# Token chunks of 368, 368 and 352 columns instead of 364, 364 and 360 in a hybrid SSD and pooling decoder step

## The chip, the cores and the metric

The kernel runs on one core of one Trainium2 chip. The metric is device time in microseconds, from runs of the whole kernel; the profile is of one execution. Engines are TensorE (PE, with its weight loads as PEld), VectorE (DVE), ScalarE (ACT), GpSimd (POOL) and SyncE (SP), which issues most DMAs.

## The reference

One inference step of a two-layer decoder trunk, on a prompt of 1024 tokens and eight sampled sequences of 8 tokens each. All 1088 tokens go through the same weights, in float32.

```
for layer 0 (SSD) and layer 1 (pooling):
    shift, scale, gate = split(silu(c) @ ada_w + ada_b, 3)
    hn = rmsnorm(x) * (1 + scale) + shift
    layer 0: zxbcdt = hn @ w_in                    # 1024 -> 6176
             xbc = silu(causal_conv4(xbc))         # carries conv state
             y, state = ssd_scan(x, dt, A, B, C)   # 32 heads, state 128, chunks of 128
             out = (groupnorm(y * silu(z))) @ w_out        # 2048 -> 1024
    layer 1: u, z = split(hn @ w_in, 2)            # 1024 -> 2 x 2048
             pooled = window means of u (2, 4, 8, 16) - u
             mixed = (pooled @ w_group) * ch_scale * silu(z)   # 4 groups of 512 -> 512
             out = mixed @ w_out                   # 2048 -> 1024
    x = x + (1 + gate) * out
y = rmsnorm(x)
```

It returns y for prompt and samples and the new SSM, convolution and pooling states.

## The kernel before, in words

Everything is held transposed: channels on the 128 partitions, the 1088 tokens along the free dimension, first the 1024 of the prompt, then the 64 of the samples. Every float32 operand of the large products is split into a high part `hi` in the reduced format fp32r and a rest `lo` in the same format, and a product of 128 input by 128 output channels is three matmuls, issued by the helper `mm1` (L182 to L184), the weights standing and the tokens streaming:

```
nc.tensor.matmul(ps[:, :n], hi[:, k, :], ah[:, a:a + n], start=first, stop=False)
nc.tensor.matmul(ps[:, :n], hi[:, k, :], al[:, a:a + n], start=False, stop=False)
nc.tensor.matmul(ps[:, :n], lo[:, k, :], ah[:, a:a + n], start=False, stop=last)
```

A PSUM tile holds at most 512 columns, so the tokens are cut into the three chunks of the constant `CH` (L20); `mm3` runs `mm1` over all input tiles k (8 or 4) of one chunk, and the chunk is then evicted. Chunk 2 ends in the 64 sample columns, which are evicted separately.

Large products come in two kinds. The *plain* ones use `CH`. The *fast* ones (`product`, L980 to L982, in `fast_pair`; and `op_half`, L1196 to L1198, in `out_product`) are a seven-product scheme on half blocks, whose streams are always a quarter of the tokens, 272 columns; they do not use `CH`. What uses `CH`:

- `front`: the first four gate tiles of the SSD input projection (8 steps of k each), the squares and the modulation of its first input tile.
- `proj_group`: 20 tiles of the SSD input projection for the groups in `BESIDE` (8 steps each). They are generators that `ssd_layer` steps between pieces of the scan (`scan_group`), by the hand-written counts in `FILL`; `proj_evict` (L419) copies a chunk out with ScalarE.
- `op_units` and `last_part`: the first output projection in four parts of four input tiles, 8 output tiles each (4 steps each); parts 0 to 2 also fill the scan's gaps. `op_unit` (L764) adds each chunk to the residual with VectorE.
- `ssd_out`: by chunk, the norm and the modulation for the second layer (`modulate`).
- `plain_pairs`: four tiles of the pooling layer's input projection (8 steps each).
- `pool_mix`: the 16 tiles of the mixer (4 steps each); L1096 multiplies a chunk into the gate.

The plain products' PSUM tiles are of the tag `mm` with three buffers (in `plain_pairs` also `y`). In the scan, `states` (L588) and `rows` (L609, L613) are TensorE's other work, and L663 runs the samples' state products, 512 columns wide in the same reduced format. The order of the engines' queues follows the order of these generators, with `issue_after` edges where the code gives one.

Of the kernel before, what the change touches and what calls it, by code (L numbers as in the profile page):

```python
# [16 lines left out]
NS = 64  # L17
TOK = NP + NS
HALF, QUART = TOK // 2, TOK // 4
CH = ((0, 364), (364, 364), (728, 360))  # L20
KD = 8
EPS = 1e-6
GROUPS = (1, 2, 3, 0)
# [74 lines left out]
class Build:  # L98
# [288 lines left out]
    def proj_group(self, G):  # L387

        for ii in range(4):
            w = self.stream_next()  # L390
            raw = self.proj_begin(G, ii)
            if (G["g"], ii) == (BESIDE[-1], 3):

                ps = [self.mm_tile() for _ in CH]
                for k in range(8):
                    for c in range(3):
                        self.mm1(ps[c], w, k, self.hn[k], CH[c], k == 0, k == 7)
                    self.slots.free(*self.hn[k])
# [9 lines left out]
            for c in range(3):  # L408
                ps = self.mm_tile()
                self.mm3(ps, w, self.hn, CH[c])  # L410
                self.proj_evict(G, ii, raw, ps, c)
# [4 lines left out]
    def proj_evict(self, G, ii, raw, ps, c):  # L416
        nc, (a, n) = self.nc, CH[c]
        pn = min(a + n, NP) - a
        nc.scalar.activation(raw[:, 3 + a:3 + a + pn], ps[:, :pn], AF.Identity)  # L419
        if pn < n:  # L420
            nc.scalar.activation(raw[:, 1027:1115].rearrange("p (b w) -> p b w", w=11)[:, :, 3:11],
                                 ps[:, pn:n].rearrange("p (b i) -> p b i", i=8), AF.Identity)
            self.proj_end(G, ii, raw, True)

    def gate_chunk(self, dst, c, ps):

        return self.z_chunk(dst, ps[:, :CH[c][1]], *CH[c])

# [343 lines left out]
    def sq_add(self, ss, x, d, first, a=0, n=TOK, eng=None):  # L772
        nc = self.nc
        eng = eng or nc.gpsimd
        if first:
            nc.scalar.activation(ss[:, a:a + n], x[:, a:a + n], AF.Square)
            return
        for b, m in CH if n == TOK else ((a, n),):
            t = self.gp2.tile([P, HALF], F32, tag="mt2", bufs=self.nmt2, name=self.name("sq"))
# [1027 lines left out]
```

## Time and profile before

| | us |
|---|---|
| runs before, median of 3 (lowest, highest) | 1631.87 (1627.06, 1631.94) |
| profiled execution, span from first to last instruction | 1632.2 |
| PE busy in it | 1601.1 (98%) |
| PEld busy | 1524.7 (93%) |
| DVE busy | 1290.3 (79%) |
| ACT busy | 816.7 (50%) |
| POOL busy | 495.2 (30%) |

For the profiled execution there is no other time than its span. Busy time counts an instruction from its start to a modelled end, and matmuls overlap in it; what a matmul takes of TensorE is read from the distance between starts. A row of the timeline has the start in us, the length in us, the engine, the line, the operation, the tile written and those read, and the shapes.

### The profile page before, as it was taken

How to read it: one execution, taken by the hardware profiler on the slowest of the kernel's cores; microseconds unless marked ns; L12 is line 12 of the kernel's file. 1: busy time of each engine (PE TensorE's matmuls, PEld its weight loads, DVE VectorE, ACT ScalarE, POOL GpSimd, SP SyncE). 2: the span in 40 equal slices, each digit the busy share in tenths (PEclk: the TensorE clock that was granted, in tenths of full speed). 3: DMA queues.
4: the chain of work that ended last, by engine and by line, in shares of the span. 5: the costliest groups of instructions: out<-in, count | busy, mean ns of one | idle time of the engine just before them, and what ended most of it. 6: DMA issues, size and time to landing. Idle time of an engine off the chain costs nothing.

```text
span 1632.2 us, 30956 instructions
## 1 busy us (share of the span) xinstructions
PE 1601.1 (98%) x12061; PEld 1524.7 (93%) x12061; DVE 1290.3 (79%) x2140; ACT 816.7 (50%) x1565; POOL 495.2 (30%) x527
## 2 busy tenths in 40 slices
PE   8999999999999999999999999999999999999997
PEld 6899999998899888988998899999999999999997
DVE  6875779777788888789887867988889867577876
ACT  6653334456776767575645536632322333333364
POOL 0233556511221202121212222366667640000241
PEclk9999999999999999999999999999999999999999
DMA  9422232264555554668898533043333369565783
GB/s 346 163 98 84 93 109 71 105 203 133 183 162 167 165 186 135 217 232 299 276 332 284 201 137 111 29 142 112 102 112 99 129 213 367 166 170 173 167 164 119
DMA packets 122306, 275.60 MB, mean 169 GB/s; under 512 B 18192, under 2 KB 59312, under 8 KB 122160
## 3 DMA queue, kind: packets, MB, share of 16 engines
q1 hardware_dynamic: 118128, 260.91, 46.8%
q0 software_dynamic: 4032, 12.72, 4.5%
q8 instruction: 95, 1.56, 0.4%
q14 instruction: 51, 0.42, 0.1%
HBM read 201.12 MB, written 70.23 MB: 166 GB/s over the span
## 4 chain that ended last, share of the span: by engine, by line
PE 82%; DVE 7%; DMA 5%; issue 3%; ACT 2%; POOL 1%; SPq 0%; DVEq 0%; ACTq 0%; POOLq 0%
PE st L982 11%; PE st L980 11%; PE st L981 11%; PE mm L182 10%; PE mm L184 10%; PE mm L183 10%; DMA acb<-acd 2%; PE op L1197 2%; PE op L1198 2%; PE op L1196 2%; PE y L609 2%; PE S L588 2%; PE y L613 2%; PE am L253 1%; PE tr L549 1%
## 5 line engine op out<-in xcount | busy, mean ns | idle before, releaser
L982 PE MATMUL st<-hh,w 128*128 128x272 f32 x832 | 240.8, 289 | 2.3 <-DVE w L176 2.3
L980 PE MATMUL st<-hh,w 128*128 128x272 f32 x832 | 240.2, 289 | 0.0
L981 PE MATMUL st<-hl,w 128*128 128x272 f32 x832 | 239.7, 288 | 0.0
L982 PE MATMUL st<-t,w 128*128 128x272 f32 x624 | 179.6, 288 | 0.0
L980 PE MATMUL st<-t,w 128*128 128x272 f32 x624 | 179.6, 288 | 0.0
L981 PE MATMUL st<-t,w 128*128 128x272 f32 x624 | 179.2, 287 | 0.0
L182 PE MATMUL mm<-hh,wh 128*128 128x364 f32 (+1 forms) x528 | 178.4, 338 | 0.1
L184 PE MATMUL mm<-hh,wl 128*128 128x364 f32 (+1 forms) x528 | 174.6, 331 | 0.0
L183 PE MATMUL mm<-hl,wh 128*128 128x364 f32 (+1 forms) x528 | 173.7, 329 | 0.0
L174 ACT ACTIVATE w<-wr 128x512 fp32r<-128x512 f32 x104 | 65.6, 631 | 190.4 <-PE st L982 156.8
L982 PEld LDWEIGHTS st<-hh,w 128*128 128x128 f32 x832 | 156.4, 188 | 3.4 <-DVE w L176 3.4
L980 PEld LDWEIGHTS st<-hh,w 128*128 128x128 f32 x832 | 156.7, 188 | 0.3 <-issue 0.3
L981 PEld LDWEIGHTS st<-hl,w 128*128 128x128 f32 x832 | 156.8, 188 | 0.0
L596 POOL TENSOR_TENSOR hd<-h,cd 128x256 f32<-128x256 f32 x56 | 47.1, 842 | 353.6 <-DVE h L597 195.4
L182 PE MATMUL mm<-gh,wh 128*128 128x364 f32 (+1 forms) x384 | 130.2, 340 | 2.1 <-ACT raw L419 2.1
L1197 PE MATMUL op<-b,w 128*128 128x272 f32 x448 | 129.0, 288 | 1.3 <-DVE b L1126 1.3
L1198 PE MATMUL op<-b,w 128*128 128x272 f32 x448 | 129.0, 288 | 0.7 <-DVE w L1170 0.7
L1196 PE MATMUL op<-b,w 128*128 128x272 f32 x448 | 129.6, 289 | 0.0
L184 PE MATMUL mm<-gh,wl 128*128 128x364 f32 (+1 forms) x384 | 127.1, 331 | 0.0
L183 PE MATMUL mm<-gl,wh 128*128 128x364 f32 (+1 forms) x384 | 126.7, 330 | 0.1
L980 PEld LDWEIGHTS st<-t,w 128*128 128x128 f32 x624 | 117.7, 189 | 0.0
L982 PEld LDWEIGHTS st<-t,w 128*128 128x128 f32 x624 | 117.3, 188 | 0.0
(293 smaller groups left out, 4613.7 us busy)
## 6 DMA issues: line engine op xcount, KB each, us to landing
wr<-win SPq DMA_DIRECT2D x48, 512.0 KB, 3.7
acb<-acd SPq DMA_DIRECT2D x64, 256.0 KB, 3.9
wr<-pin SPq DMA_DIRECT2D x32, 512.0 KB, 3.6
wr<-pout SPq DMA_DIRECT2D x28, 512.0 KB, 3.9
x<-x1d SPq DMA_DIRECT2D x24, 544.0 KB, 6.3
x1d<-x SPq DMA_DIRECT2D x22, 544.0 KB, 5.4
wr<-pout POOLq DMA_DIRECT2D x20, 512.0 KB, 5.5
x<-xT SPq DMA_DIRECT2D x16, 544.0 KB, 6.0
```

The source lines that it names most:

```text
L174: self.nc.scalar.activation(hi, src, AF.Copy)
L182: nc.tensor.matmul(ps[:, :n], hi[:, k, :], ah[:, a:a + n], start=first, stop=False)
L183: nc.tensor.matmul(ps[:, :n], hi[:, k, :], al[:, a:a + n], start=False, stop=False)
L184: nc.tensor.matmul(ps[:, :n], lo[:, k, :], ah[:, a:a + n], start=False, stop=last)
L588: nc.tensor.matmul(S[:, 256 * i:256 * i + 256], Bt, xde.rearrange("p r q -> p (r q)"), start=True, stop=True)
L596: nc.gpsimd.tensor_tensor(out=hd, in0=h[-1], in1=cd.unsqueeze(2).to_broadcast([P, 4, 64]), op=ALU.mult)
L980: nc.tensor.matmul(ps[c][:, :QUART], hi[:, k], xh[:, t], start=(k == 0), stop=False)
L981: nc.tensor.matmul(ps[c][:, :QUART], hi[:, k], xl[:, t], start=False, stop=False)
L982: nc.tensor.matmul(ps[c][:, :QUART], lo[:, k], xh[:, t], start=False, stop=(k == 3))
L1196: nc.tensor.matmul(ps[:, :QUART], hi[:, k], xh, start=k == 0, stop=False)
L1197: nc.tensor.matmul(ps[:, :QUART], hi[:, k], xl, start=False, stop=False)
L1198: nc.tensor.matmul(ps[:, :QUART], lo[:, k], xh, start=False, stop=k == 7)
```

## The change

One constant. The three chunks start at columns 0, 368 and 736 instead of 0, 364 and 728, and are 368, 368 and 352 columns wide instead of 364, 364 and 360. All loops over `CH` follow it; their number of steps stays.

```
-CH = ((0, 364), (364, 364), (728, 360))
+CH = ((0, 368), (368, 368), (736, 352))
```

## The prediction

> **What bounds the kernel now.** I read first the shares on the page, then the chain that ended last, then the groups of matmuls by shape, and last the timeline of the stretches in which the chunked products run.
>
> ```profile
> span 1632.2 us, 30956 instructions
> PE 1601.1 (98%) x12061; PEld 1524.7 (93%) x12061; DVE 1290.3 (79%) x2140; ACT 816.7 (50%) x1565; POOL 495.2 (30%) x527
> PEclk9999999999999999999999999999999999999999
> PE 82%; DVE 7%; DMA 5%; issue 3%; ACT 2%; POOL 1%; SPq 0%; DVEq 0%; ACTq 0%; POOLq 0%
> ```
>
> TensorE is busy for 1601.1 of 1632.2 us at an undiminished granted clock, and 82% of the chain is TensorE. So a change is worth what it does to TensorE's start-to-start times, and 31 us of idle time is all that better cover could still win. Three lines of the helper `mm1` (L182 to L184) issue every matmul that the change touches. Their groups, one shape apart from the other:
>
> ```profile
> L182 PE MATMUL mm<-hh,wh 128*128 128x364 f32 x352 | 119.0, 338 | 0.1
> L182 PE MATMUL mm<-hh,wh 128*128 128x360 f32 x176 | 59.4, 338 | 0.0
> L182 PE MATMUL mm<-gh,wh 128*128 128x364 f32 x256 | 87.1, 341 | 2.1 <-ACT raw L419 2.1
> L182 PE MATMUL mm<-gh,wh 128*128 128x360 f32 x128 | 43.3, 338 | 0.0
> ```
>
> The mean of one (338 ns) overlaps its neighbours, since the ends are modelled, and is no price. Two things are to be seen: the two widths come two to one, and TensorE hardly waits before them (0.1 and 2.1 us in total). Priced by starts: a stretch of the pooled mixer, where nothing else runs on TensorE, taken at the first matmul of each change of width (24 of 364 columns, 12 of 360, 24 of 364, 12 of 360):
>
> ```profile
> 1358.75 0.33 PE L182 MATMUL mm<-ph,wh 128*128 128x364 f32 x1
> ...
> 1362.74 0.33 PE L182 MATMUL mm<-ph,wh 128*128 128x360 f32 x1
> ...
> 1364.75 0.33 PE L182 MATMUL mm<-ph,wh 128*128 128x364 f32 x1
> ...
> 1368.74 0.33 PE L182 MATMUL mm<-ph,wh 128*128 128x360 f32 x1
> ...
> 1370.70 0.33 PE L182 MATMUL mm<-ph,wh 128*128 128x364 f32 x1
> ```
>
> A 364-column matmul costs 3.99 us / 24 = 166.25 ns, both times. A 360-column one costs 2.01 / 12 = 167.5 ns the first time and 1.96 / 12 = 163.3 ns the second. So 360 columns have two gaits, 4.2 ns apart, and in the slower one four columns less are no cheaper at all. One matmul of each of the three chunks together is 11.95 us / 72 x 3 = 497.9 ns. That the two gaits are no accident of this stage is seen in the SSD input projection (24 matmuls each; the first and the last of them):
>
> ```profile
> 409.95 0.33 PE L183 MATMUL mm<-hl,wh 128*128 128x360 f32 x1
> ...
> 413.54 0.33 PE L184 MATMUL mm<-hh,wl 128*128 128x360 f32 x1
> ```
>
> ```profile
> 500.98 0.33 PE L183 MATMUL mm<-hl,wh 128*128 128x360 f32 x1
> ...
> 504.64 0.33 PE L184 MATMUL mm<-hh,wl 128*128 128x360 f32 x1
> ```
>
> Those are 22 intervals each: 3.59 / 22 = 163.2 ns and 3.66 / 22 = 166.4 ns.
>
> **The change part by part.** The number of instructions stays on every engine: three chunks before, three after, the third still ending in the 64 sample columns (288 + 64 instead of 296 + 64). By the code's loops (4 + 20 + 4 tiles of 8 steps, and 32 + 16 of 4 steps, three matmuls a step) there are 416 x 3 = 1248 matmuls of each chunk; L182's rows above are 912 of its 1248 over all three. So the whole question is what 368 + 368 + 352 costs against 497.9 ns, 1248 times over. No 368 or 352 stands in the trace; the nearest widths are these, the only ones that run in the same number format:
>
> ```profile
> 1200.01 0.29 PE L980 MATMUL st<-t,w 128*128 128x272 f32 x1
> ...
> 1202.64 0.29 PE L980 MATMUL st<-hh,w 128*128 128x272 f32 x1
> ```
>
> ```profile
> 419.31 0.39 PE L663 MATMUL S<-xs,Bt 128*128 128x512 f32 x1
> ...
> 420.00 0.40 PE L663 MATMUL S<-xs,Bl 128*128 128x512 f32 x1
> ```
>
> 272 columns cost 2.63 us / 21 = 125.2 ns, 512 cost 0.69 / 3 = 230 ns. Three ways to read the price of 368 and 352 out of this:
>
> Steps of 16 columns. 272 and 512 are multiples of 16, 368 and 352 as well; 360 and 364 are not, and both would be charged as 368. That is what the slower gait of 360 looks like (166.4 to 167.5 against 166.25). Then 368 costs what 364 costs, 166.25; a step is (166.25 - 125.2) / 6 = 6.84 ns; 352 costs 159.4. The sum is 491.9, so 6.0 ns less, and 1248 x 6.0 = 7.5 us.
>
> By the column, on the best line. From 272 to the fast 360 it is (163.3 - 125.2) / 88 = 0.433 ns a column: 368 costs 166.8, 352 costs 159.8, sum 493.4, 4.5 ns less, 5.6 us.
>
> By the column, through 364. It is 41.05 / 92 = 0.446 ns: 368 costs 168.0, 352 costs 160.9, sum 496.9, 1.0 ns or 1.2 us less. Through 512 (104.8 / 240 = 0.437) 368 is 167.2 and 352 160.2, sum 494.6, 4.1 us less.
>
> I take the first. Its nearest row is 364: the width that is closest to 368, twice as frequent as 360, and steady at 166.25 in both passes. The ends are 1.2 and 7.5 us of gain, and the other side is the second rival.
>
> How much of it lies on the path is read by stages:
>
> ```profile
> 355.00:720.00 365.00, 363.61 (x2842) 327.29 (x2842) 292.01 (x453) 251.59 (x578) 68.29 (x131) 1.00 0.54 175
> 720.00:955.00 235.00, 228.40 (x1691) 210.75 (x1690) 197.21 (x356) 127.32 (x284) 38.71 (x36) 0.99 0.78 270
> 955.00:1058.00 103.00, 99.92 (x584) 96.03 (x583) 80.33 (x156) 60.02 (x122) 30.03 (x40) 1.00 0.25 87
> 1352.00:1450.00 98.00, 97.97 (x595) 97.58 (x594) 69.28 (x99) 32.91 (x40) 7.04 (x7) 1.00 0.68 223
> ```
>
> After the span come in order: elapsed time, TensorE, weight loads, VectorE, ScalarE, GpSimd. TensorE idles for 1.4 of 365 us in the input projection, for 0.03 of 98 us in the mixer, but for 6.6 of 235 us where the first output projection fills the scan's gaps. There the last groups of the scan wait for other engines and DMAs, and a quicker matmul only lengthens the wait behind it. I take a tenth off for that: 7.5 x 0.9 = 6.7 us.
>
> The evictions move by four columns:
>
> ```profile
> L419 ACT ACTIVATE raw<-mm 128x364 f32<-128x364 f32 x40 | 18.7, 468 | 12.0 <-PE mm L184 11.5
> L419 ACT ACTIVATE raw<-mm 128x296 f32<-128x296 f32 x20 | 8.2, 409 | 6.6 <-PE mm L184 6.3
> ```
>
> That is 59 ns for 68 columns, 0.87 a column: a first or second chunk's eviction grows by 3.5 ns, the third's prompt part shrinks by 7, and the totals are equal. It lies beside the next chunk's matmuls: three PSUM buffers take turns, and a chunk of 24 matmuls lasts 4 us. Were that cover gone it would be 3.5 ns on each of 152 long chunks (two in each of the 76 weight tiles), 0.5 us. The chunked modulation between the layers goes the same way: the first chunk comes some ns later, the last some ns earlier. Both I cost at nothing. DMAs are of whole tiles in the chunked stages, but for the residual's last columns, whose pieces shift by 16 to 32 bytes a row; I cost that at nothing, as the outgoing store is waited for only one stage later.
>
> Sum: 1632.2 - 6.7 = 1625.5 us by the profiled execution. The median of the runs, 1631.87, is 0.3 us from that span, so it stands for both.
>
> **The rivals.** *Time goes by columns alone.* 1088 columns stay 1088. By the line through 364 the gain is 1.2 us, of which 1.1 reach the end: about 1631 us, no change that can be told. For it speaks that 272, 364 and 512 lie within 1.5 ns of one line; against it, that 360 lies on the line in one gait only. The Trainium skill, in "TensorE: Matmul & The Clock Gate", section "Wait — 56ns, not 53.3ns?", has such a rule: warm starts follow at columns ÷ 2.4 GHz plus about 2.5 ns. By it the three chunks would be 460.8 ns before and after and the change worth nothing. The trace does not agree on the size (497.9), and 360 costing as much as 364 is against the form, but its 2.5 ns was measured in another format.
>
> *The new widths fall into the slower gait.* The place is the same 3744 matmuls. On the best line (0.433) plus the 4.2 ns between the gaits, 368 would cost 171.0 and 352 164.0: a sum of 506.0, 8.1 ns more, 10.1 us, and 1642 us, since a slower TensorE is on the path everywhere. It makes the kernel slower by over 0.3% once the sum passes 497.9 + 4.9 us / 1248 = 501.8, that is, with more than about two thirds of the matmuls in that gait. For it: nothing in the rows tells what selects the gait, and 360 takes it in most passes. Against it: 364 shows a steady 166.25, and 272, a multiple of 16 as the new widths are, stays at 125.
>
> *The order around the matmuls shifts.* The build lays the engines' orders out from the program's lengths; a DMA or split placed later in the scan stage or in the last products opens waits such as these:
>
> ```profile
> PE S L588 <- ACT Bt L566: 4.5, 3, 2.3
> PE mm L182 <- ACT raw L419: 2.1, 1, 2.1
> ```
>
> Three more waits of 2 us, with no gain elsewhere, give 1638 us; together with the forecast's gain they give about 1631.
>
> **How the numbers follow.** The steps of 16 get 0.46, the columns alone (with a gain that waits eat up) 0.26, the slower gait 0.18 and the shifted order 0.10. What a measurement can tell from no change is 0.3%, 4.9 us. So faster 0.46, same 0.26, slower 0.28. The forecast is 1625.5. The three runs before spread over 4.9 us (1627.06 to 1631.94); the low end is the undiminished gain, 1624.4, less that spread: 1619.5. The high end takes in the shifted order and most of the slower gait: 1640. The likeliest case alone would be 1621 to 1629.
>
> **What would show it.** Right: in the mixer the 24 matmuls of 368 columns take 3.99 us and the 12 of 352 take 1.91, and no width has two gaits; the mixer's stretch, 98 us with 576 such matmuls, shortens by about 1.1 us, the input projection's, with 1440, by about 2.9. Wrong: 368 at 168 and 352 at 161 (columns alone), 368 near 171 (the gait), or TensorE's idle time above 34 us with prices as forecast (the order).

## The result and the profile after

| | before | after |
|---|---|---|
| median (lowest to highest), 15 runs each | 1631.18 us (1627.06 to 1634.55) | 1626.04 us (1622.69 to 1631.28) |
| ratio after / before, 95% interval | | 0.9971 [0.9962, 0.9980] |
| span of the profiled execution | 1632.2 us | 1623.2 us |

The kernel became faster by 0.29%, about 4.7 us by the ratio and 5.1 by the medians. The two profiled executions lie 9.0 us apart, more than the medians do; the last experiment tells why. The page after:

```profile
span 1623.2 us, 30975 instructions
PE 1594.8 (98%) x12061; PEld 1519.9 (94%) x12061; DVE 1290.4 (79%) x2140; ACT 815.2 (50%) x1565; POOL 497.8 (31%) x527
PEclk9999999999999999999999999999999999999999
PE 83%; DVE 6%; DMA 4%; issue 3%; ACT 3%; POOL 1%; SPq 0%; DVEq 0%; POOLq 0%; ACTq 0%
```

Each of the five engine rows counts as many instructions as before; VectorE and ScalarE were as busy as before (1290.3 and 816.7 us then). TensorE's busy time fell by 6.3 us, and it is as much the bound as it was. The pooled mixer in the timeline, at each change of width (start in us, length, line, operation, shape):

```profile
1346.58 0.33 PE L182 MATMUL mm<-ph,wh 128*128 128x368 f32 x1
...
1350.61 0.32 PE L182 MATMUL mm<-ph,wh 128*128 128x352 f32 x1
...
1352.51 0.33 PE L182 MATMUL mm<-ph,wh 128*128 128x368 f32 x1
```

24 matmuls of 368 columns take 4.03 us, 167.9 ns each; 12 of 352 take 1.90 us, 158.3 ns. The three chunks together cost 5.93 us / 36 x 3 = 494.2 ns, where they cost 497.9. So 368 is dearer than 364 was, and the gain comes from the third chunk.

### The profile page after: what moved, and what is told of

The parts are those of the page before. It is cut to its first block, busy times and chain, and to the rows that moved or that the text cites. A ratio compares the mean times of both kernels' runs of the same rounds, so it can differ in the third digit from the quotient of the medians.

```text
span 1623.2 us, 30975 instructions
## 1 busy us (share of the span) xinstructions
PE 1594.8 (98%) x12061; PEld 1519.9 (94%) x12061; DVE 1290.4 (79%) x2140; ACT 815.2 (50%) x1565; POOL 497.8 (31%) x527
## 4 chain that ended last, share of the span: by engine, by line
PE 83%; DVE 6%; DMA 4%; issue 3%; ACT 3%; POOL 1%; SPq 0%; DVEq 0%; POOLq 0%; ACTq 0%
PE st L982 11%; PE st L980 11%; PE st L981 11%; PE mm L182 10%; PE mm L183 10%; PE mm L184 10%; PE op L1197 2%; PE op L1198 2%; PE op L1196 2%; PE y L609 2%; PE S L588 2%; PE y L613 1%; DMA acb<-acd 1%; PE am L253 1%; PE tr L549 1%
## 5 line engine op out<-in xcount | busy, mean ns | idle before, releaser
L182 PE MATMUL mm<-hh,wh 128*128 128x368 f32 (+1 forms) x528 | 178.2, 338 | 0.1
L183 PE MATMUL mm<-hl,wh 128*128 128x368 f32 (+1 forms) x528 | 173.4, 328 | 0.0
L184 PE MATMUL mm<-hh,wl 128*128 128x368 f32 (+1 forms) x528 | 173.4, 328 | 0.0
L182 PE MATMUL mm<-gh,wh 128*128 128x368 f32 (+1 forms) x384 | 129.1, 337 | 0.6 <-ACT raw L419 0.6
L183 PE MATMUL mm<-gl,wh 128*128 128x368 f32 (+1 forms) x384 | 126.0, 328 | 1.1 <-DVE gl L743 1.0
L184 PE MATMUL mm<-gh,wl 128*128 128x368 f32 (+1 forms) x384 | 126.0, 328 | 0.0
```

## The experiments

A *gait* is one of several start-to-start times that a matmul of one width can keep for a whole chunk. The theories: *steps of 16 columns*, on which the forecast stood; *columns alone*; *gaits*, where some widths or starts are dearer than the line through the others; and the *order* of the work around the matmuls, or its luck from execution to execution.

### Price lists

The kernel before, and behind its last output store one group of 24 matmuls after another (32 groups in the first list, 149 in the second), from one pair of token tiles and one weight tile.

```
+        self.price(rst, x)          # after the last scale(...)
...
+        for i, (a, n) in enumerate(PRICE):
+            ps = self.op_tile()
+            for k in range(8):
+                self.mm1(ps, (wk, wk), k, (hi, lo), (a, n), k == 0, k == 7)
```

> The kernel before, and behind its last output store 31 groups of 24 matmuls of the helper mm1, one group after the other, each at one width and one start: 19 widths from 256 to 512 at start 0, then 360, 364, 368 and 352 at several starts. Their results are not used. Start to start within a group, by theory: Steps of 16 columns: 356, 360, 364 and 368 cost the same (about 166 to 168 ns), 340 to 352 the same (about 159), a stair with treads of 16 columns and 6.8 ns rise. Columns alone: a straight line of 0.44 ns a column, 352 at 160.5, 360 at 164, 364 at 166, 368 at 167.5. Two gaits: the straight line for most widths, and 360 (perhaps other widths that are no multiple of 16) some 3 to 4 ns above it; if the start selects the gait, 360 at start 728 is slow and at start 0 or 368 fast. Start: 368 at start 368 costs 1 to 2 ns more than at 0, as in the changed kernel.

Measured, in the timeline the first row of each group at start 0:

```profile
1655.18 0.32 PE L183 MATMUL op<-ph,pv 128*128 128x352 f32 x1
...
1659.05 0.33 PE L183 MATMUL op<-ph,pv 128*128 128x356 f32 x1
...
1662.89 0.32 PE L183 MATMUL op<-ph,pv 128*128 128x360 f32 x1
...
1666.84 0.33 PE L183 MATMUL op<-ph,pv 128*128 128x364 f32 x1
...
1670.83 0.33 PE L183 MATMUL op<-ph,pv 128*128 128x368 f32 x1
...
1674.84 0.33 PE L183 MATMUL op<-ph,pv 128*128 128x372 f32 x1
```

The distances are 24 matmuls each: 161.3 ns for 352 columns, 160.0 for 356, 164.6 for 360, 166.3 for 364, 167.1 for 368. There is no stair: 356 costs no more than 352, and 360 lies between. Nor is it a line. Taken from the third matmul of a group on, the same list has 360 columns at 164.4 ns at starts 0 and 4, but at 166.7 at starts 8 and 368 and 166.6 at 728; 368 at 166.8 at start 0, 169.0 at 368, 166.7 at 720; 352 at 161.1 at start 0 and 158.3 at 736. Width and start together set the price, over some 2 to 3 ns.

> As the first price list, with 149 groups of 24 matmuls behind the last output store: widths 332 to 400 at start 0, 105 pairs of a first chunk (336 to 384) and a second chunk's width at the start that follows from it, the 20 third chunks that are left, and 256, 260, 264, 280 at start 0. If start and width together fix the price, the starts and widths that the first list had come out as there within 0.5 ns (364 at 0: 166.4; 364 at 364: 165.8; 368 at 368: 169.0; 352 at 736: 158.3; 360 at 728: 166.6). If the gait is chance, they differ by up to 4 ns. Columns alone: 0.44 ns a column everywhere. Steps of 16: a stair. 256 columns at half the rate again (213 ns) if that belongs to the width, and about 118 ns if it was the first group's start-up.

The second list had these prices again: 364 at 364 165.8, 368 at 368 169.1, 352 at 736 158.3 and, repeated at its end, 158.5; 360 at 728 166.8 and 166.5. Only 352 at start 0 missed, with 159.8 where the first list had 161.1. The groups take turns on six PSUM tiles, and these repeats of 360 at 728 and of 352 at 736 stood behind other groups and, one of them in each case, on another tile; so for these neither the tile nor the group ahead sets the price. 256 columns cost 120.0 ns, so the 213 ns of the first list was its first group's start-up. 368 and 372 columns at start 344, then 352 at 736, 348 at 740 and 344 at 744:

```profile
1760.35 0.33 PE L183 MATMUL op<-ph,pv 128*128 128x368 f32 x1
...
1764.49 0.34 PE L183 MATMUL op<-ph,pv 128*128 128x372 f32 x1
...
2170.16 0.32 PE L183 MATMUL op<-ph,pv 128*128 128x352 f32 x1
...
2173.96 0.32 PE L183 MATMUL op<-ph,pv 128*128 128x348 f32 x1
...
2177.64 0.32 PE L183 MATMUL op<-ph,pv 128*128 128x344 f32 x1
```

At start 344, 368 columns cost 4.14 / 24 = 172.5 ns, 5.4 more than at 0. At 740, 348 columns cost 3.68 / 24 = 153.3, 5.0 less than 352 at 736 for four columns. The chunks before add up to 499.3 ns in this list, those after to 494.1.

### The widths in another order, and other widths

```
-CH = ((0, 364), (364, 364), (728, 360))
+CH = ((0, 352), (352, 368), (720, 368))    # first kernel
+CH = ((0, 372), (372, 372), (744, 344))    # second
+CH = ((0, 384), (384, 384), (768, 320))    # third
```

> Chunks of 352, 368 and 368 columns: the changed kernel's widths in another order. If the widths' prices make the gain, it stays: ratio to the kernel before 0.997 (0.996 to 0.998). If the gain is an accident of the order in which the other engines' work falls around the chunks, it goes: ratio about 1.000.

> Chunks of 372, 372 and 344 columns, starts 0, 372 and 744. Steps of 16 columns: 24 + 24 + 22 = 70 steps against 69 before and 68 in the changed kernel, so 6.8 ns times 1248 more than before, 8 us: ratio 1.005. Columns alone: ratio 1.000. Two gaits, where only 360 is dear: ratio 0.998; where any width that is no multiple of 16 can be, 1.000.

> Chunks of 384, 384 and 320 columns, all multiples of 32, starts 0, 384 and 768. Steps of 16 columns: 24 + 24 + 20 = 68 steps as in the changed kernel: ratio 0.997. Two gaits with multiples of 16 in the good one: 0.997 too. Columns alone: 1.000.

Measured: 0.9957 [0.9943, 0.9970], 1.0000 [0.9989, 1.0012] and 0.9986 [0.9973, 0.9998]. The first keeps the gain, so it is no accident of one order. The second has by the stair one step of 16 more than before and is not slower. The third has the changed kernel's 68 steps and about half its gain.

### One boundary alone

```
+CH = ((0, 368), (368, 360), (728, 360))    # the first boundary
+CH = ((0, 364), (364, 372), (736, 352))    # the second
```

> Only the first boundary of the change: chunks of 368, 360 and 360 columns at 0, 368 and 728. By the first price list 166.8 + 166.7 + 166.6 = 500.1 ns, 1.3 more than before's 498.8 (166.4 + 165.8 + 166.6): 1.6 us slower, ratio 1.001. Steps of 16: 69 steps, as before: 1.000. If the first boundary made the gain: 0.997.

> Only the second boundary of the change: chunks of 364, 372 and 352 columns at 0, 364 and 736. By the price lists 166.4 + about 170 (372 at 0 cost 170.0; at 364 unknown) + 158.3 = 494.7, 4.1 ns less than before, 5.1 us: ratio 0.997. Steps of 16: 23 + 24 + 22 = 69 as before: 1.000.

Measured: 1.0000 [0.9988, 1.0012] and 0.9988 [0.9979, 0.9998]. The first came out as the list (1.001) and the steps (1.000) both allow, and without the gain (0.997); the second kept less than half of what the list promised. Its mixer shows why:

```profile
1346.30 0.33 PE L182 MATMUL mm<-ph,wh 128*128 128x364 f32 x1
...
1348.32 0.33 PE L182 MATMUL mm<-ph,wh 128*128 128x372 f32 x1
...
1350.37 0.32 PE L182 MATMUL mm<-ph,wh 128*128 128x352 f32 x1
...
1352.36 0.33 PE L182 MATMUL mm<-ph,wh 128*128 128x364 f32 x1
```

352 columns at start 736 take 1.99 us / 12 = 165.8 ns here, against 158.3 in the changed kernel's mixer. Width and start are the same, so a gait exists beside the list's price. What ran just before does not settle it: the last tiles of the same mixer, behind the same 364 and 372 columns, have the fast gait (1.90 / 12 = 158.3).

```profile
1424.71 0.33 PE L182 MATMUL mm<-ph,wh 128*128 128x364 f32 x1
...
1426.71 0.33 PE L182 MATMUL mm<-ph,wh 128*128 128x372 f32 x1
...
1428.75 0.32 PE L182 MATMUL mm<-ph,wh 128*128 128x352 f32 x1
...
1430.65 0.33 PE L182 MATMUL mm<-ph,wh 128*128 128x364 f32 x1
```

### The cheapest and the dearest chunks of the list

```
+CH = ((0, 384), (384, 356), (740, 348))    # cheapest
+CH = ((0, 356), (356, 384), (740, 348))    # the same widths, two exchanged
+CH = ((0, 344), (344, 368), (712, 376))    # dearest
```

> The cheapest three chunks of the second price list: 384, 356 and 348 columns at 0, 384 and 740, listed at 173.3 + 160.1 + 153.3 = 486.8 ns, against 499.3 for the chunks before (166.7 + 165.8 + 166.8 in the same list). If the gain is the price of each width at its start, 12.5 ns times 1248 = 15.6 us at most, ratio 0.990 (0.992 if the gait in the kernel is not the list's everywhere). Steps of 16: 24 + 23 + 22 = 69 steps as before, ratio 1.000. Columns alone: 1.000. Only multiples of 16 in the good gait: two of the three are none, 1.000 or slower.

> The same widths with the first two in the other order: 356, 384 and 348 columns at 0, 356 and 740, listed at 160.0 + 174.9 + 153.3 = 488.2 ns, 11.1 ns less than before, 13.9 us: ratio 0.9915 by the price list. Steps of 16 and columns alone: 1.000.

> The dearest three chunks of the second price list: 344, 368 and 376 columns at 0, 344 and 712, listed at 157.8 + 173.1 + 172.8 = 503.7 ns, 4.4 more than before, 5.5 us: ratio 1.0033. Steps of 16: 22 + 23 + 24 = 69 as before, 1.000. Columns alone: 1.000.

Measured: 0.9955 [0.9941, 0.9970], 0.9959 [0.9946, 0.9971] and 1.0018 [1.0006, 1.0030]. All three have 69 steps of 16 and 1088 columns, as before; two are faster and one is slower, each on the list's side. The mixers of the cheapest and of the dearest:

```profile
1352.51 0.34 PE L182 MATMUL mm<-ph,wh 128*128 128x384 f32 x1
...
1354.59 0.32 PE L182 MATMUL mm<-ph,wh 128*128 128x356 f32 x1
...
1356.51 0.32 PE L182 MATMUL mm<-ph,wh 128*128 128x348 f32 x1
...
1358.37 0.34 PE L182 MATMUL mm<-ph,wh 128*128 128x384 f32 x1
```

```profile
1356.64 0.32 PE L182 MATMUL mm<-ph,wh 128*128 128x344 f32 x1
...
1358.51 0.33 PE L182 MATMUL mm<-ph,wh 128*128 128x368 f32 x1
...
1360.54 0.34 PE L182 MATMUL mm<-ph,wh 128*128 128x376 f32 x1
...
1362.61 0.32 PE L182 MATMUL mm<-ph,wh 128*128 128x344 f32 x1
```

5.86 us for 36 matmuls is 488.3 ns for the three chunks of the first, 5.97 us is 497.5 for the second in this stretch, its first tile (499 in the tiles behind it). The gain of the cheapest is half of what the list gave. The kernel's prices were higher than the list's (348 at 1.86 / 12 = 155.0 ns, not 153.3), and by the table below perhaps not all of them reached the end.

All kernels side by side. The sum is that of the three chunks' mean start-to-start times in the kernel's own profile (all distances under 200 ns within a chunk, more than 900 for each; another choice of the distances that count moves a sum by up to 0.5 ns); by price is its difference to 497.8 ns, times 1248; measured is (ratio - 1) x 1630 us.

| chunks | sum, ns | by price, us | measured, us |
|---|---|---|---|
| 368, 368, 352 (the change) | 494.9 | -3.6 | -4.7 |
| 352, 368, 368 | 493.9 | -4.9 | -7.0 |
| 372, 372, 344 | 499.3 | +1.9 | 0.0 |
| 384, 384, 320 | 494.6 | -4.0 | -2.3 |
| 368, 360, 360 | 498.9 | +1.4 | 0.0 |
| 364, 372, 352 | 497.9 | +0.1 | -2.0 |
| 384, 356, 348 | 490.0 | -9.7 | -7.3 |
| 356, 384, 348 | 491.0 | -8.5 | -6.7 |
| 344, 368, 376 | 500.5 | +3.4 | +2.9 |

But for two pairs of neighbours, the price sets the order of the kernels; what is left over is up to 2.4 us either way, and the intervals are some 2 us to each side.

### Both kernels once more

> The kernel before, unchanged, for a second profile. In the first one the stage of the last products lasted 183.5 us and the first output projection 272.1 us, in the changed kernel 181.3 and 268.1, while the prices of the matmuls explain none and about 1 us of that. If the rest belongs to the build (the order of the queues), it is there again: 183 to 184 and 271 to 273. If it belongs to the execution, the two stages come out elsewhere, nearer 181 and 269, with the prices by chunk as before (166.4, 165.7, 165.6).

> The changed kernel, unchanged, for a second profile. By the build: last products 181.3 us, first output projection 268. By the execution: they move by 2 us or more. The prices by chunk stay (167.0, 168.7, 159.2), if they belong to width and start.

Both were single runs, with no interval: 1631.59 and 1627.52 us, spans 1629.8 and 1625.6. The sums of the three chunks came back to 0.1 ns (497.8 before, 494.9 after), so a kernel's mean price belongs to the program. The gait of a single chunk does not. In the mixer of before, 360 columns alternate from tile to tile between 163.3 and about 167.5 ns. Up to a wait in the fourth tile the two executions have the same gaits; the wait is not the same in both, and behind it they are out of step. The third chunk of the fifth tile, first execution, then second:

```profile
1380.97 0.33 PE L182 MATMUL mm<-ph,wh 128*128 128x360 f32 x1
...
1382.93 0.33 PE L182 MATMUL mm<-ph,wh 128*128 128x364 f32 x1
```

```profile
1380.77 0.33 PE L182 MATMUL mm<-ph,wh 128*128 128x360 f32 x1
...
1382.78 0.33 PE L182 MATMUL mm<-ph,wh 128*128 128x364 f32 x1
```

1.96 / 12 = 163.3 ns in one, 2.01 / 12 = 167.5 in the other, for the same instructions on the same tiles in the same order. So the gait depends on the course of the execution up to the chunk. Both gaits come equally often in this stretch, and the mean stays.

By stage, from the first matmul of each to that of the next (the two profiles of each kernel). The work ahead of the first row (354.8 to 357.2 us) and the plain pairs between the second and the third (53.7 to 54.3) are left out: there the two profiles of before differ by more than the kernels' means.

| stage | before, us | after, us | by price, us |
|---|---|---|---|
| SSD input projection beside the scan | 376.6, 376.1 | 374.8, 375.4 | -1.5 |
| first output projection | 272.1, 270.5 | 268.0, 267.0 | -0.9 |
| fast products of the pooling layer | 295.0, 295.0 | 295.0, 295.0 | none |
| mixer | 95.9, 95.8 | 95.3, 95.4 | -0.6 |
| last products and norm | 183.5, 181.3 | 181.3, 181.6 | none |

The rows behind the second line, first profile before, then first after, are the first matmul of the stage and the first of the next (the number in brackets is the wait ahead of it, in us); after, three rows of the scan's small matmuls stand ahead of the stage:

```profile
732.00 0.43 PE L182 MATMUL mm<-gh,wh 128*128 128x364 f32 x1 [2.06 <-ACT raw L419]
...
1004.06 0.33 PE L182 MATMUL pl<-hh,wh 128*128 128x364 f32 x1
```

```profile
728.08 0.38 PE L545 MATMUL tr<-xbc,xbc 128*128 128x128 f32 x2
728.30 0.49 PE L549 MATMUL tr<-kc,xbc 128*128 128x128 f32 x3
728.54 0.48 PE L663 MATMUL S<-xs,Bt 128*128 128x512 f32 x1
729.61 0.43 PE L182 MATMUL mm<-gh,wh 128*128 128x368 f32 x1 [0.59 <-ACT raw L419]
...
997.65 0.33 PE L182 MATMUL pl<-hh,wh 128*128 128x368 f32 x1
```

The 2.2 us of the last products were luck of the first execution of before: the second had 181.3.

The boundary between the first two stages is not at the same work in both kernels: before, these six small matmuls run behind it (the two of L545 at 733.27). So the two stages are taken together. They last 648.6 and 646.5 us before, 642.8 and 642.5 after: 4.9 less in the mean, of which the prices explain 2.4. TensorE's idle time in the first output projection is the same in the mean (4.7 and 4.5 us before, 4.8 and 4.0 after, without the wait ahead of its first matmul). The distances between matmuls that are no chunk's, the scan's above all, add up to 66.6 and 65.6 us there before and 63.4 and 63.6 after, part of it the six matmuls that moved; the slow switches within chunks (a distance of 200 ns or more) are 56 and 50 before, 48 and 46 after. Between the kernels the order of the records differs (13 of VectorE's 2140 stand elsewhere), between two executions of one kernel it does not. That the price is not behind the other 2.5 us is also seen in the kernel with chunks of 372, 372 and 344: its prices are above those of before, and its profile has the two stages at 644.0 us. That the order makes them is the reading that fits; no run fixed the order and changed the widths alone, so it is argued and not shown.

## Why the prediction was right, and where it was not

It forecast 1625.5 us and faster by 6.7; it came out at 1626.0 and faster by 4.7 (ratio) to 5.1 (medians). The sum fits better than its terms, and that is luck: the gain was put 1.6 to 2.0 us too high, and the span that it was taken from lies 1.0 us above the median of the 15 runs before.

*The bound.* Right. Times follow TensorE's start-to-start distances: the mixer, which has hardly any idle time, moved by its price, and the input projection nearly so (1.3 of 1.5 us, with six small matmuls more in it).

*The price of the new widths.* This term was mis-sized: 6.0 ns and 7.5 us forecast, 2.9 ns and 3.6 us measured. 368 was taken to cost what 364 costs, 166.25; it costs 167.9 in the mixer. 352 was taken at 159.4 and costs 158.3 to 159.2. The step that failed is the choice of the first reading: the list has no steps of 16. 360 charged like 364 was real, but it is one of two gaits of 360 at start 728, not a width rounded up. The readings by the column were nearer: 4.1 us through 512, 5.6 on the best line, 1.2 through 364. (Of the rows that it shows from the input projection, the first is the second of its 24 matmuls; the 22 intervals are right.)

*The tenth taken off.* Wrong in sign: the two stages beside the scan gained 4.9 us, not less than the 2.4 of their prices. This made up for most of the price's error, and the prediction had the shifted order as a loss alone.

*The rivals.* Columns alone is excluded: the interval of the change ends at 0.9980, and three kernels with the same 1088 columns lie at 0.9955, 0.9959 and 1.0018. In this format the three chunks cost 490 to 500 ns, by the split. The Trainium skill's rule in "TensorE: Matmul & The Clock Gate", section "Wait — 56ns, not 53.3ns?" (columns ÷ 2.4 GHz plus about 2.5 ns) would give 460.8 for any split; the traces do not agree with it here. The slower gait is real, and the dearest chunks show that it can turn the sign (500.5 ns, slower by 0.18%), but the new widths do not fall into it as a whole: 352 at 736 mostly shows 158 to 159 in the changed kernel, some chunks 162.6, and two, each behind a long first distance (251 and 248 ns), 166.7. The shifted order is there as well (the six matmuls), and by the reading above on the side of the gain; TensorE's idle time over the span, 28.4 us after, stays under the 34 that were its sign.

*Evictions and modulation at nothing.* VectorE's and ScalarE's busy times (1290.4 and 815.2 us) are those of before within 1.5 us. Their cover was not taken away in any run.

*What would show it.* The mixer's 12 matmuls of 352 columns took 1.90 us, as said (1.91); its 24 of 368 took 4.03 and not 3.99. The mixer's stretch shortened by 0.5 us where 1.1 was said, the input projection's by 1.3 where 2.9 was said. That no width would have two gaits was wrong.

## What to carry to other kernels

Where TensorE is the bound and a split of columns is free, price each chunk by the distance of starts in a clean stretch, at its own start, and add up; equal numbers of columns are not equal times, and a group of 24 matmuls per candidate behind the kernel's end gives the list in one run. Try the split that the list gives before trusting any rule of multiples, and expect less than the listed difference: by the second list the change should have gained 6.5 us and gained 4.7, the cheapest chunks 15.6 and 7.3, and 384, 384 and 320 columns 7.5 and 2.3. A chunk's gait in the kernel need not be the list's. A profile pair can overstate a change by several us of waits that have nothing to do with it: compare the stages that the change doesn't touch first.

## What was not expected of the hardware

The distance of starts of a matmul in this format, with a weight load before each, depends on the start column as well as on the width: 368 columns cost 166.8 ns at start 0, 169.0 at 368 and 172.5 at 344. At starts 0 and 384 the prices of most widths agree (360 columns: 164.5 and 164.4; 364: 166.7 and 166.4; 376: 173.5 and 173.5). Four columns can cost nothing (352 and 356 at start 0) or 5 ns (348 at 740, 352 at 736). The same chunk can settle in two gaits 4 to 8 ns apart: 352 at 736 at 158.3 or at 165.8 to 166.7, and 360 at 728 at 163.3 or 167.5, there even for the same instructions in two executions of one program, after a wait had fallen otherwise. What in the chip makes it so stays open.
